# Two transformer blocks on one core: transfers of a recurrence queued by hand, weights asked for three blocks ahead, and a reworked quarter-product stage

## The chip, the cores and the metric

One of the eight cores of a Trainium2 chip runs the kernel. The metric is the device time of one execution in microseconds (us). TensorE is written PE (its weight loads PEld), VectorE DVE, ScalarE ACT, GpSimd POOL and SyncE SP. SP computes nothing: it issues transfers, in the order of its queue. ACT also issues transfers, between its computing instructions.

## The reference

Input x has 1024 tokens of 1024 features, all in float32. Two blocks follow each other.

```
h  = x + norm(mixer(norm(x)));  h = h + norm(w_down(gelu(conv(w_up.norm(h))_gate) * conv(..)_up))
mixer: p = xn @ w_in; a gated 3-tap convolution on 512 columns; on the rest a recurrence per head (8 heads of 64):
   S_t = S_(t-1) * w_t + (S_(t-1) . -kk_t) (kk_t a_t) + v_t k_t ;   y_t = S_t r_t
second block: sliding-window attention and forgetting attention, gates, w_mix_out,
   h = h + relu(u @ w_ff1)^2 @ w_ff2;  h = h + sigmoid(norm(h) @ w_ple_gate) * (p @ w_ple_proj);  norm(h)
```

## The kernel before, in words

**Dense products.** Activations are feature-major: a tile is 128 features by 512 tokens (one of two halves). Each float32 factor is split into a high and a low part (`split`: ACT writes the high part, DVE or POOL subtracts it), and a product is three matmuls: high by high, high by low, low by high. A weight block of 128 output columns (512 KB) is loaded by SP into one of two `wr` tiles (`raw_w`, L155), split into one of two `wh` and two `wl` tiles (`load_w`, L148) and used for 24 matmuls per half (`mm3`, L160). Each block asks for its weights when it starts.

**The first stage** is one TensorE order that `weave` writes by hand. Threads yield estimated TensorE time or a `gap` in us; the clock of `weave` runs the first thread in its list that is ready. The chain of the recurrence comes first, dense products fill in (`fill`, L1567 on). The other engines are ordered by the compiler's scheduler, from its own simulated times, with what was written first going first among what is ready. The recurrence has eight units (four pairs of heads by two halves). Unit i goes through

- `pre` (L552): five loads (sig, kt, aa, rt, vt) from DRAM, DVE and ACT work, two small sums on TensorE. `pre_thread` starts it when `solve` of unit i-1 is done;
- `solve` (L605): 32 products psA, masked by DVE into `am`; the small triangular blocks go to DRAM (d_l, L632) and come back copied to four groups of partitions (lt, L634); TensorE transposes (psB, psV) meanwhile; POOL inverts (`triangle`, L665, 62 multiplications and additions); the inverse goes to DRAM (d_m, four transfers, L656; d_n, L659) and back into `am` (L661). `solve` writes all these at once; it starts when the chain of unit i-2 is done;
- `chain` (L688): `weave` lets it start 35 us (`tri`) after `solve`; it loads `tr` from d_n (four transfers, L696), does 32 small products psR, then eight serial steps psX, psU, psH, psy, whose results go through DVE (xz, hb) and ACT (uv, hw);
- `post` (L769): a norm, then a gate `gg` loaded by SP.

**The quarter products.** In both feed-forward layers the last 17 (first) and 13 (second) pairs of weight blocks use seven products of half size in place of eight (`Quads`, L882). `operands` adds high and low parts of x back together on POOL (r, L904), forms four differences T1 to T4 on DVE (L907) and splits them. `weights` forms four sums and differences of a pair of weight blocks on POOL (s, L921) and splits five quarters. `pair` asks for its weights, then writes seven products of 12 matmuls into three banks of the tag `mm` (which has three), psX, psY and psZ, each taken out by ACT or added by DVE. The scheduler orders TensorE here.

Of the kernel before, what the change touches and what calls it, by code (L numbers as in the profile page):

```python
# [21 lines left out]
DC = math.exp(-0.5)  # L22
NEG = -1.0e30
ROW = 1 / 2210
GAP = dict(rsqrt=5.0, rstd=10.0, pre=16.0, pre2=10.0, tri=35.0, mix=3.5, hid=4.0, hop=1.2, x=1.4, u=0.9, h=1.2, sol=1.2, post=4.0, post2=4.0)
CH1 = (4, 4, 4, 2, 8)
# [51 lines left out]
class Kernel:  # L78
    def __init__(self, ctx, tc, vec):
        nc = self.nc = tc.nc  # L80
        self.in_block = False
# [66 lines left out]
    def load_w(self, wd, m, kb=8, cols=128, engine=None):  # L148

        raw = self.raw_w(wd, m, kb, cols)  # L150
# [19 lines left out]
    def dense(self, wd, m, x, then, kb=8, halves=(0, 1), cols=128, engine=None):  # L170
# [7 lines left out]
        self.in_block = False  # L178

    def dense32(self, wd, x, then, halves=(0, 1)):  # L180

        nc = self.nc
        yield until(lambda: not self.in_block)
        self.in_block = True
        raw = self.raw_w(wd, 0, NB, 32)
        w = self.wp.tile([128, NB, 64], F32R, tag="wh", name="wh")
        nc.scalar.copy(out=w[:, :, 0:32], in_=raw)
        nc.vector.tensor_tensor(out=w[:, :, 32:64], in0=raw, in1=w[:, :, 0:32], op=ALU.subtract)
        for hf in halves:
# [80 lines left out]

    def norm_to(self, src, gname, waits=(GAP["rstd"], GAP["rsqrt"]), pool=()):

# [3 lines left out]
        for j in range(NB):  # L276
# [81 lines left out]
def hs(hf):  # L358
    return slice(H * hf, H * hf + H)
# [14 lines left out]
class Mixer:  # L374
# [230 lines left out]
    def solve(self, st):  # L605
# [24 lines left out]
        d_l, d_m, d_n = self.d_l[ui], self.d_m[ui], self.d_n[ui]  # L630
        for b in range(2):
            nc.sync.dma_start(out=d_l[b].rearrange("u i t -> i u t"), in_=amu[32 * b:32 * b + 32, :, 32 * b:32 * b + 32])  # L632
        lt = k.q("lt", shape=(128, 32, 32))
        nc.sync.dma_start(  # L634
            out=lt.rearrange("p i t -> p (i t)"), in_=bass.AP(d_l.tensor, d_l.offset, [[0, 4], [1024, 32], [1, 1024]]))

# [14 lines left out]
        for p in range(2):  # L651
            nc.scalar.copy(out=uv[64:128, p:7 + p:2], in_=ps[64 * p:64 * p + 64])
        mt = self.triangle(lt)

        for r in range(4):
            nc.sync.dma_start(out=d_m[:, :, :, r].rearrange("b u s t -> (b u) s t"), in_=mt[32 * r:32 * r + 32])  # L656
        nm = k.a("mk", [128, 32, 8], name="nm")
        nc.gpsimd.tensor_copy(nm, mt.rearrange("p s t -> p t s"))
        nc.sync.dma_start(out=d_n.rearrange("r u t s -> (r u) t s"), in_=nm)  # L659
        for b in range(2):  # L660
            nc.sync.dma_start(  # L661
                out=amu[32 * b:32 * b + 32, :, 32 * b:32 * b + 32], in_=d_m[b].rearrange("u s r t -> (s r) u t"))
        return ar, am, bt, uv, wc, bv, d_n

# [23 lines left out]
    def chain(self, u, st):  # L688
        k = self.k
        nc = k.nc  # L690
        j, hf = u
        ar, am, bt, uv, wcs, bv, d_n = st
        amu = am.rearrange("p c h t -> p (c h) t")
        tr = k.a("tr", [64, 16, 4, 8])
        for r in range(4):
            nc.sync.dma_start(out=tr[0:32, :, r], in_=d_n[r, 0:16].rearrange("u t s -> t u s"))  # L696
        ps = k.ps("sc", (128, 16, 32), "psR")
# [184 lines left out]
class Quads:  # L882
# [6 lines left out]

    def operands(self, x):  # L890

# [74 lines left out]
class Ffn:  # L966
# [20 lines left out]
    def quads(self, js, q):  # L987
# [3 lines left out]
        pairs = self.up.pairs(js)  # L991
        for blocks, m0, m1 in pairs:
            cs = yield from q.pair(self.up.w, m0, m1)
            if blocks == pairs[-1][0]:
                self.hidden(0, (0, 1), "ws")
            self.up.pair(blocks, cs, keep)
# [474 lines left out]
def tile_blocks(ctx, tc, a, out):  # L1471
# [3 lines left out]
    ya_d, yb_d, h_d, h2_d, h3_d = d("ya_d", 4), d("yb_d", 4), d("h_d", 8), d("h2_d", 8), d("h3_d", 8)  # L1475
    sw_d, fx_d, gt_d, pj_d = d("sw_d", 4), d("fx_d", 4), d("gt_d", 16), d("pj_d", 8)
    xn = [{} for _ in range(NB)]

# [74 lines left out]
    def w_out_norm(src, hf):  # L1553
        yield from k.norm_add(src, "post_mix_g", a["x"], hf)
        k.spill(src, h_d, hf)
        yield gap(10.0)
        prs = yield from k.norm_to(src, "pre_ffn_g")
        for j, p in enumerate(prs):
# [3 lines left out]
    def krv(j, hf, names="krv"):  # L1562
        yield from mixer.krv(j, xn, (hf,), names)
        if "v" in names:
            done.add(("krv", (j, hf)))

    def fill():  # L1567
        kept = {}
        for token in ORDER:
# [38 lines left out]
    with tc.manual_schedule(engines={mybir.EngineType.PE}):  # L1608
        weave([*[chain_thread(i) for i in range(8)], post_thread(), pre_thread(), solve_thread(), norms(), norm0(), tail(),
               ple(), fill()])  # L1610
    k.a.close("mix")
    k.a.close("mixc")

    def ffn(ff, x, first, n):

        k.a.open("quad", QUAD, "right")
        q = Quads(k)
        q.operands(x)
# [7 lines left out]

    ffn(ff1, ff_in, 5, 22)

# [30 lines left out]
    for hf in range(2):  # L1659
        src = run(br.run(ys[hf], hf))  # L1660
        if hf == 0:
            ys.append(br.load(1))
        for j, p in enumerate(run(k.norm_to(src, "g_mlp_2"))):
            ff_in2[j][hf] = p
    run(ff2.ups(range(6), ff_in2, (0,)))
    k.a.close("q")
    k.a.close("att")
    ffn(ff2, ff_in2, 6, 32)
    pl_in = [{} for _ in range(NB)]
# [93 lines left out]
```

## Time and profile before

| | us |
|---|---|
| median of 3 runs (lowest, highest) | 3073.11 (3060.45, 3076.32) |
| the profiled execution's own time | 3067.94 |
| its span, first to last instruction | 3066.2 |
| TensorE busy in the span | 2883.5 (94%) |
| VectorE, ScalarE, GpSimd busy | 1822.0, 1260.5, 1003.5 |
| mean granted TensorE clock | 0.969 |

An instruction of an engine waits until what it needs is there, and everything behind it on that engine's queue waits too. `[idle before <-releaser]` in a timeline row is the time that the engine stood idle before the instruction, and who ended that wait. "Granted clock" is TensorE's clock as a share of 2.4 GHz; 0.5 is the lower level, 1.2 GHz.

### The profile page before, as it was taken

The numbers are of one execution on the slowest core, as the hardware profiler recorded it, in microseconds if no ns is written. First come the engines' busy times: TensorE is split into PE (matmuls) and PEld (weight loads), VectorE is DVE, ScalarE is ACT, GpSimd is POOL, SyncE is SP. The second block draws the span as 40 slices with busy tenths as digits, with TensorE's granted clock in tenths as the row PEclk, the third lists the DMA queues.
The fourth block names the chain that finished last, engine by engine and source line by source line (L and its number), as shares of the span: only waits on it lengthen the run. The fifth ranks groups of instructions, "written<-read, shape, count | busy, mean of one in ns | idle before, by whom it ended". The sixth has DMA issues, their size and how long they took to land.

```text
span 3066.2 us, 39452 instructions
## 1 busy us (share of the span) xinstructions
PE 2883.5 (94%) x14392; PEld 2316.4 (76%) x14392; DVE 1822.0 (59%) x3244; ACT 1260.5 (41%) x2187; POOL 1003.5 (33%) x1056
## 2 busy tenths in 40 slices
PE   7978889988998999999999999989998999999997
PEld 5756667766776777788778888877887787888886
DVE  6545555446886666445645776786667443544476
ACT  6433323234544444413335665564334443212342
POOL 2152433321345443003453446560026541000343
PEclk8988899999999999999999999999999999999998
DMA  6544332324422223423442322226543334433323
GB/s 209 173 116 121 106 99 75 90 66 158 162 87 83 82 76 100 147 66 96 152 163 64 91 73 73 73 66 223 165 134 114 117 110 145 172 98 102 97 89 131
DMA packets 188194, 349.72 MB, mean 114 GB/s; under 512 B 58712, under 2 KB 69464, under 8 KB 188000
## 3 DMA queue, kind: packets, MB, share of 16 engines
q1 hardware_dynamic: 146368, 268.51, 28.8%
q10 hardware_dynamic: 41632, 78.69, 7.0%
q8 instruction: 113, 1.85, 0.3%
q14 instruction: 81, 0.66, 0.1%
HBM read 265.05 MB, written 82.08 MB: 113 GB/s over the span
## 4 chain that ended last, share of the span: by engine, by line
PE 59%; DVE 6%; POOL 2%; issue 2%; DMA 2%; ACT 2%; ACTq 0%; SPq 0%; DVEq 0%; POOLq 0%
PE ps_mm L165 39%; PE psX L935 9%; PE psZ L935 5%; PE psY L935 2%; POOL s L921 1%; DVE sq L255 1%; PE pso L1326 1%; PE pst L1319 1%; DMA wr<-in_w_ff 1%; PE pso L1243 0%; PE pss L1280 0%; PE pss L1281 0%; DVE T L907 0%; DVE wl L146 0%; PE pst L1238 0%
## 5 line engine op out<-in xcount | busy, mean ns | idle before, releaser
L145 ACT CAST wh<-wr 128x1024 fp32r<-128x1024 f32 (+2 forms) x343 | 318.2, 928 | 647.2 <-PE ps_mm L165 534.2
L165 PE MATMUL ps_mm<-xh,wh 128*128 128x512 f32 x1344 | 547.2, 407 | 4.5 <-ACT xh L145 1.7
L165 PE MATMUL ps_mm<-xl,wh 128*128 128x512 f32 x1344 | 543.0, 404 | 1.8 <-DVE xl L146 1.8
L146 POOL TENSOR_TENSOR wl<-wr,wh 128x1024 fp32r<-128x1024 f32 (+1 forms) x109 | 255.2, 2342 | 853.6 <-ACT wh L145 671.2
L165 PE MATMUL ps_mm<-xh,wl 128*128 128x512 f32 x1344 | 370.5, 407 | 0.0
L165 PE MATMUL ps_mm<-hh,wh 128*128 128x512 f32 x864 | 343.2, 397 | 8.7 <-DVE acc L1029 3.8
L165 PE MATMUL ps_mm<-hl,wh 128*128 128x512 f32 x864 | 342.9, 397 | 0.0
L146 DVE TENSOR_TENSOR wl<-wr,wh 128x1024 fp32r<-128x1024 f32 (+2 forms) x234 | 250.5, 1071 | 107.2 <-PE ps_mm L165 45.8
L165 PEld LDWEIGHTS ps_mm<-xh,wh 128*128 128x128 f32 x1344 | 257.6, 192 | 62.4 <-issue 2.1
L165 PEld LDWEIGHTS ps_mm<-xl,wh 128*128 128x128 f32 x1344 | 257.5, 192 | 55.6 <-DVE xl L146 2.3
L165 PEld LDWEIGHTS ps_mm<-xh,wl 128*128 128x128 f32 x1344 | 251.1, 192 | 54.0
L1029 DVE TENSOR_TENSOR acc<-acc,ps_mm 128x512 f32<-128x512 f32 x176 | 120.6, 686 | 248.4 <-PE ps_mm L165 241.5
L165 PE MATMUL ps_mm<-hh,wl 128*128 128x512 f32 x864 | 233.8, 396 | 0.0
L677 POOL TENSOR_TENSOR pr<-mt,lt 128x60 f32<-128x60 f32 (+24 forms) x248 | 96.9, 391 | 328.7 <-DMA lt<-d_l 309.9
L165 PEld LDWEIGHTS ps_mm<-hh,wh 128*128 128x128 f32 x864 | 163.8, 190 | 48.5 <-DVE acc L1029 4.2
L165 PEld LDWEIGHTS ps_mm<-hl,wh 128*128 128x128 f32 x864 | 163.9, 190 | 38.2
L165 PEld LDWEIGHTS ps_mm<-hh,wl 128*128 128x128 f32 x864 | 163.4, 189 | 38.2
L921 POOL TENSOR_TENSOR s<-wr 128x512 f32<-128x512 f32 x60 | 90.2, 1503 | 272.0 <-DMA wr<-in_w_up 148.5
L255 DVE TENSOR_TENSOR sq<-sq 128x512 f32<-128x512 f32 x112 | 123.5, 1102 | 36.5 <-ACT sq L253 24.2
L904 POOL TENSOR_TENSOR r<-xh,xl 128x512 f32<-128x512 f32 x32 | 70.0, 2215 | 229.4 <-PE ps_mm L165 177.1
L1303 POOL TENSOR_SCALAR S<-S,sm 128x512 f32<-128x512 f32 (+3 forms) x96 | 119.2, 1253 | 73.8 <-DVE sm L1301 48.5
L805 DVE SCALAR_TENSOR_TENSOR ft<-c,vec,ft 128x1023 f32<-128x1023 f32 x68 | 92.1, 1355 | 40.6 <-ACT ft L803 40.4
(379 smaller groups left out, 5824.5 us busy)
## 6 DMA issues: line engine op xcount, KB each, us to landing
wr<-in_w_in SPq DMA_DIRECT2D x58, 512.0 KB, 4.0
wr<-in_w_up SPq DMA_DIRECT2D x54, 512.0 KB, 3.5
h<-hid SPq DMA_DIRECT2D x108, 256.0 KB, 4.2
wr<-in_w_ff SPq DMA_DIRECT2D x54, 512.0 KB, 3.5
wr<-in_w_in2g SPq DMA_DIRECT2D x32, 512.0 KB, 3.5
hid<-c ACTq DMA_DIRECT2D x26, 512.0 KB, 2.8
wr<-in_w_ff SPq DMA_DIRECT2D x48, 256.0 KB, 2.7
hid<-ft ACTq DMA_DIRECT2D x17, 512.0 KB, 2.6
```

Of the source, the lines that this page charges most:

```text
L145: self.nc.scalar.copy(out=pair[0], in_=src)
L146: (engine or self.nc.vector).tensor_tensor(out=pair[1], in0=src, in1=pair[0], op=ALU.subtract)
L165: self.nc.tensor.matmul(ps, lhsT=a[:, j, :cols], rhs=x[j][hf][part], start=i == 0, stop=i == 3 * kb - 1)
L255: self.nc.vector.tensor_tensor(out=sq, in0=acc, in1=sq, op=ALU.add)
L677: e.tensor_tensor(out=pr, in0=mt[:, :n, i:i + 1].to_broadcast([128, n, m]), in1=lt[:, i:i + 1, i + 1:].to_broadcast([128, n, m]), op=ALU.mult)
L805: nc.vector.scalar_tensor_tensor(out=t[:, i:], in0=src[:, :-i], scalar=c(2 - i), in1=t[:, i:], op0=ALU.mult, op1=ALU.add)
L904: nc.gpsimd.tensor_tensor(out=raw[n], in0=pr[0], in1=pr[1], op=ALU.add)
L921: nc.gpsimd.tensor_tensor(out=o, in0=x, in1=y, op=op)
L935: self.k.nc.tensor.matmul(ps, lhsT=a[:, j], rhs=x[j][part], start=start and i == 0, stop=i == 3 * half - 1, skip_group_check=True)
L1029: k.nc.vector.tensor_tensor(out=o, in0=o, in1=ps, op=ALU.add)
L1303: nc.gpsimd.tensor_scalar(out=s, in0=s, scalar1=sums[0], scalar2=None, op0=ALU.mult)
L1319: nc.tensor.transpose(pt[:, x], sc[i, e][kb // 4][:, c0:c0 + 128], k.ident)
```

## The change

It has three parts. **Weights:** `fill` writes a plan of its weight blocks; asking for one block also asks for the next ones, so that three stand ahead. **Recurrence:** the transfers are written at other places and tied on SP's queue behind the weight load written last (`queued`); the inverse's way back is a thread of its own; `pre` of unit i may start when `solve` of unit i-2 is done. **Quarters:** `norm_to` also stores x whole in DRAM, `operands` loads it instead of adding, two of four differences move to POOL, weights of the next pair are asked for before a pair's products, psY takes a bank of another tag, and TensorE follows the written order from the `ups` before them on.

```diff
-GAP = dict(... tri=35.0, ...)
+AHEAD = 3
+GAP = dict(... tri=3.0, ... dl=3.0, inv=28.0, back=4.0, ...)
...
     def load_w(self, wd, m, kb=8, cols=128, engine=None):
+        def get(wd, m):
+            if wd.shape[-1] == 32:
+                return self.fetch32(wd)
+            return self.fetch(wd, m, kb, cols, engine)
+        asked = [x for x in (self.ahead[:1] or self.plan[:1]) if x[0] is wd and x[1] == m]
+        if not asked:
+            return get(wd, m)
+        w = self.ahead.pop(0)[2] if self.ahead else get(*self.plan.pop(0))
+        while self.plan and len(self.ahead) < AHEAD:
+            nxt = self.plan.pop(0)
+            self.ahead.append((*nxt, get(*nxt)))
+        return w
...
-        self.nc.sync.dma_start(out=raw, in_=wd[m])
+        self.last_load = self.nc.sync.dma_start(out=raw, in_=wd[m])
+    def queued(self):
+        return self.tc.issue_after(getattr(self.last_load, "ins", self.last_load))
...
             self.split(x, pr, nc.gpsimd if j in pool else nc.vector)
+            if keep is not None:
+                nc.scalar.dma_start(out=keep[0][j][:, hs(keep[1])], in_=x)
...
-        for b in range(2):
-            nc.sync.dma_start(out=d_l[b]..., in_=amu[...])
-        lt = k.q("lt", shape=(128, 32, 32))
-        nc.sync.dma_start(out=lt..., in_=bass.AP(d_l.tensor, d_l.offset, [[0, 4], [1024, 32], [1, 1024]]))
+        with k.queued():
+            for b in range(2):
+                nc.sync.dma_start(out=d_l[b]..., in_=amu[...])
...
-        mt = self.triangle(lt)
-        for r in range(4):
-            nc.sync.dma_start(out=d_m[:, :, :, r]..., in_=mt[32 * r:32 * r + 32])
+        yield gap(GAP["dl"])
+        lt = k.q("lt", shape=(128, 32, 32))
+        with k.queued():
+            nc.sync.dma_start(out=lt..., in_=bass.AP(d_l.tensor, d_l.offset, [[0, 4], [1024, 32], [1, 1024]]))
+        return ar, am, bt, uv, wc, bv, self.triangle(lt), (d_m, d_n)
+    def back(self, st):
...
+        yield gap(GAP["inv"])
         nm = k.a("mk", [128, 32, 8], name="nm")
         nc.gpsimd.tensor_copy(nm, mt.rearrange("p s t -> p t s"))
-        nc.sync.dma_start(out=d_n..., in_=nm)
-        for b in range(2):
-            nc.sync.dma_start(out=amu[...], in_=d_m[b]...)
+        with k.queued():
+            for r in range(4):
+                nc.sync.dma_start(out=d_m[:, :, :, r]..., in_=mt[32 * r:32 * r + 32])
+            nc.sync.dma_start(out=d_n..., in_=nm)
+        yield gap(GAP["back"])
+        tr = k.a("tr", [64, 16, 4, 8])
+        with k.queued():
+            for b in range(2):
+                nc.sync.dma_start(out=amu[...], in_=d_m[b]...)
+            for r in range(4):
+                nc.sync.dma_start(out=tr[0:32, :, r], in_=d_n[r, 0:16]...)
+        return *st, tr
...
     def chain(self, u, st):
-        tr = k.a("tr", [64, 16, 4, 8])
-        for r in range(4):
-            nc.sync.dma_start(out=tr[0:32, :, r], in_=d_n[r, 0:16]...)
...
     def operands(self, x, x_d):
-            for n, pr in (("11", x[i][0]), ("12", x[i][1]), ("22", x[half + i][1]), ("21", x[half + i][0])):
-                raw[n] = k.t("r" + n, tag="ws")
-                nc.gpsimd.tensor_tensor(out=raw[n], in0=pr[0], in1=pr[1], op=ALU.add)
+            for n, j, hf in (("11", i, 0), ("12", i, 1), ("22", half + i, 1), ("21", half + i, 0)):
+                raw[n] = k.load(x_d[j], hf, "r" + n, "ws")
...
-                nc.vector.tensor_tensor(out=raw[n], in0=raw[a], in1=raw[b], op=ALU.subtract)
+                e = nc.gpsimd if n in ("T3", "T4") else nc.vector
+                e.tensor_tensor(out=raw[n], in0=raw[a], in1=raw[b], op=ALU.subtract)
...
-    def pair(self, wd, m0, m1):
-        w = self.weights(wd, m0, m1)
-        px, py, pz = [k.ps("mm", name=n) for n in ("psX", "psY", "psZ")]
+    def pair(self, w):
+        px, py, pz = [k.ps(tag, name=n) for tag, n in (("mm", "psX"), ("sc", "psY"), ("mm", "psZ"))]
...
     def quads(self, js, q):
-        for blocks, m0, m1 in pairs:
-            cs = yield from q.pair(self.up.w, m0, m1)
+        ws = [q.weights(self.up.w, *pairs[0][1:])]
+        for i, (blocks, _, _) in enumerate(pairs):
+            if i + 1 < len(pairs):
+                ws.append(q.weights(self.up.w, *pairs[i + 1][1:]))
+            cs = yield from q.pair(ws.pop(0))
...
     def pre_thread():
-            yield has(("krv", u), ("rate", u), *([("solve", i - 1)] if i > 1 else []))
+            yield has(("krv", u), ("rate", u), *([("solve", i - 2)] if i > 2 else []))
...
+    def back_thread():
+        for i in range(8):
+            yield has(("solve", i))
+            solved[i] = yield from mixer.back(solved[i])
+            done.add(("back", i))
     def chain_thread(i):
-        yield has(("solve", i))
+        yield has(("back", i))
...
     def ffn(ff, x, x_d, first, n):
-        run(ff.ups(range(first), x, (1,)))
-        run(ff.quads(range(first, n), q))
+        with tc.manual_schedule(engines={mybir.EngineType.PE}):
+            run(ff.ups(range(first), x, (1,)))
+            run(ff.quads(range(first, n), q))
```

## Rows read from the trace of the kernel before

**Rows 1.** Busy time by engine (share of the span, instructions), the page.

```profile
PE 2883.5 (94%) x14392; PEld 2316.4 (76%) x14392; DVE 1822.0 (59%) x3244; ACT 1260.5 (41%) x2187; POOL 1003.5 (33%) x1056
```

**Rows 2.** Busy time and granted clock in stretches, core 0 (x: instructions).

```profile
core 0: us, PE busy (x) PEld busy (x) DVE busy (x) ACT busy (x) POOL busy (x), PEclk, DMA share, GB/s
0.00:730.00 730.00, 621.62 (x4165) 481.81 (x4166) 381.75 (x817) 273.30 (x505) 222.33 (x583) 0.90 0.40 119
...
862.00:968.00 106.00, 95.24 (x393) 74.62 (x392) 81.30 (x101) 51.41 (x76) 47.16 (x30) 0.97 0.27 90
968.00:1248.00 280.00, 271.21 (x1162) 216.90 (x1161) 177.71 (x169) 130.20 (x178) 112.25 (x72) 1.00 0.25 81
...
2327.00:2415.00 88.00, 79.41 (x333) 63.00 (x333) 50.20 (x52) 38.96 (x62) 52.02 (x37) 0.98 0.31 104
2415.00:2600.00 185.00, 182.64 (x792) 148.21 (x790) 76.62 (x89) 76.38 (x111) 60.75 (x43) 1.00 0.34 117
```

**Rows 3.** TensorE's waits from 0 to 740 us: total, times, longest.

```profile
PE psH L745 <- ACT uv L742: 30.0, 6, 13.0
PE psB L643 <- DVE am L624: 16.1, 1, 16.1
PE psR L699 <- DMA tr<-d_n: 13.9, 3, 5.9
PE ps_mm L165 <- ACT wh L145: 12.1, 2, 8.1
PE psl L439 <- DVE wax L456: 8.1, 1, 8.1
```

**Rows 4.** Waits of SP's queue from 0 to 740 us.

```profile
SPq L656 <- POOL mt L680: 107.3, 7, 19.0
```

**Rows 5.** Timelines of SP (first two) and DVE about 180 us.

```profile
170.89 2.60 SPq L656 DMA_DIRECT2D d_m<-mt  x4
...
179.53 0.43 SPq L140 DMA_DIRECT2D sig<-d_sig  x1
...
183.00 0.43 DVE L564 TENSOR_SCALAR sig<-sig 128x512 f32<-128x512 f32 x1 [16.92 <-DMA sig<-d_sig]
```

**Rows 6.** Timeline of ACT and of its transfers about 231 us.

```profile
231.17 0.34 ACTq L443 DMA_DIRECT2D d_sig<-lo  x1
...
236.36 0.69 ACT L442 ACTIVATE lo<-psl,hw 128x512 f32<-128x512 f32 x1 [13.90 <-DMA am<-d_m]
```

**Rows 7.** One unit from lt to psR: timelines of SP, POOL and PE.

```profile
467.96 0.56 SPq L634 DMA_DIRECT2D lt<-d_l  x1
...
506.18 2.53 SPq L656 DMA_DIRECT2D d_m<-mt  x4
...
478.14 0.24 POOL L677 TENSOR_TENSOR pr<-mt,lt 128x31 f32<-128x31 f32 x1 [30.28 <-DMA lt<-d_l]
...
515.02 2.02 PE L699 MATMUL psR<-tr,am 32*32 32x32 f32 x32 [5.94 <-DMA tr<-d_n]
```

**Rows 8.** Busy time and granted clock just after that wait, columns of rows 2.

```profile
515.00:527.00 12.00, 11.92 (x98) 9.76 (x98) 4.12 (x6) 5.52 (x11) 0.00 (x0) 0.52 0.45 154
```

**Rows 9.** Transfers by issue: KB each, median us from issue to landing.

```profile
wr<-in_w_in SPq DMA_DIRECT2D x58, 512.0 KB, 4.0
```

**Rows 10.** Timeline of PE: one quarter product of two successive pairs.

```profile
1008.08 0.50 PE L935 MATMUL psZ<-T1h,S1h 128*128 128x512 f32 x1 [0.68 <-ACT c L962]
...
1028.40 0.50 PE L935 MATMUL psZ<-T1h,S1h 128*128 128x512 f32 x1 [0.68 <-ACT c L962]
```

**Rows 11.** POOL's sums of x (the page); from 968 to 1248 us: two DVE splits, POOL.

```profile
L904 POOL TENSOR_TENSOR r<-xh,xl 128x512 f32<-128x512 f32 x32 | 70.0, 2215 | 229.4 <-PE ps_mm L165 177.1
...
L146 DVE TENSOR_TENSOR S1l<-s,S1h 128x512 fp32r<-128x512 f32 x12 | 17.2, 1430 | 36.1 <-ACT S1h L145 36.1
...
L146 DVE TENSOR_TENSOR S4l<-s,S4h 128x512 fp32r<-128x512 f32 x12 | 8.1, 679 | 0.0
...
L921 POOL TENSOR_TENSOR s<-wr,s 128x512 f32<-128x512 f32 x12 | 15.6, 1300 | 0.9
```

More of the change, by code (lines that the diff above doesn't have):

```diff
@@ L23 @@
 NEG = -1.0e30
+AHEAD = 3
 ROW = 1 / 2210
-GAP = dict(rsqrt=5.0, rstd=10.0, pre=16.0, pre2=10.0, tri=35.0, mix=3.5, hid=4.0, hop=1.2, x=1.4, u=0.9, h=1.2, sol=1.2, post=4.0, post2=4.0)
+GAP = dict(rsqrt=5.0, rstd=10.0, pre=16.0, pre2=10.0, tri=3.0, mix=3.5, hid=4.0, hop=1.2, x=1.4, u=0.9, h=1.2, sol=1.2, dl=3.0, inv=28.0, back=4.0, post=4.0, post2=4.0)
 CH1 = (4, 4, 4, 2, 8)
@@ L80, in __init__ @@
         nc = self.nc = tc.nc
+        self.tc = tc
+        self.last_load = None
+        self.plan, self.ahead = [], []
         self.in_block = False
@@ L178, in dense, with fetch32 @@
         self.in_block = False
+    def fetch32(self, wd):
+        nc = self.nc
+        raw = self.raw_w(wd, 0, NB, 32)
+        w = self.wp.tile([128, NB, 64], F32R, tag="wh", name="wh")
+        nc.scalar.copy(out=w[:, :, 0:32], in_=raw)
+        nc.vector.tensor_tensor(out=w[:, :, 32:64], in0=raw, in1=w[:, :, 0:32], op=ALU.subtract)
+        return w
     def dense32(self, wd, x, then, halves=(0, 1)):
@@ L184, in dense32 @@
         self.in_block = True
[L185 to L188, printed above, removed]
+        w = self.load_w(wd, 0)
         for hf in halves:
@@ L269, in rstd_of, with norm_to @@
         return r
-    def norm_to(self, src, gname, waits=(GAP["rstd"], GAP["rsqrt"]), pool=()):
+    def norm_to(self, src, gname, waits=(GAP["rstd"], GAP["rsqrt"]), pool=(), keep=None):
         nc = self.nc
@@ L630, in solve @@
         d_l, d_m, d_n = self.d_l[ui], self.d_m[ui], self.d_n[ui]
[L631 to L635 removed]
+        with k.queued():
+            for b in range(2):
+                nc.sync.dma_start(
+                    out=d_l[b].rearrange("u i t -> i u t"), in_=amu[32 * b:32 * b + 32, :, 32 * b:32 * b + 32])
         bt = k.q("bt", shape=(128, 8, 128))
@@ L652, in solve @@
             nc.scalar.copy(out=uv[64:128, p:7 + p:2], in_=ps[64 * p:64 * p + 64])
[L653 to L656 removed]
+        yield gap(GAP["dl"])
+        lt = k.q("lt", shape=(128, 32, 32))
+        with k.queued():
+            nc.sync.dma_start(
+                out=lt.rearrange("p i t -> p (i t)"),
+                in_=bass.AP(d_l.tensor, d_l.offset, [[0, 4], [1024, 32], [1, 1024]]))
+        return ar, am, bt, uv, wc, bv, self.triangle(lt), (d_m, d_n)
+    def back(self, st):
+        k = self.k
+        nc = k.nc
+        *st, mt, (d_m, d_n) = st
+        amu = st[1].rearrange("p c h t -> p (c h) t")
+        yield gap(GAP["inv"])
         nm = k.a("mk", [128, 32, 8], name="nm")
         nc.gpsimd.tensor_copy(nm, mt.rearrange("p s t -> p t s"))
[L659 to L663 removed]
+        with k.queued():
+            for r in range(4):
+                nc.sync.dma_start(
+                    out=d_m[:, :, :, r].rearrange("b u s t -> (b u) s t"), in_=mt[32 * r:32 * r + 32])
+            nc.sync.dma_start(out=d_n.rearrange("r u t s -> (r u) t s"), in_=nm)
+        yield gap(GAP["back"])
+        tr = k.a("tr", [64, 16, 4, 8])
+        with k.queued():
+            for b in range(2):
+                nc.sync.dma_start(
+                    out=amu[32 * b:32 * b + 32, :, 32 * b:32 * b + 32], in_=d_m[b].rearrange("u s r t -> (s r) u t"))
+            for r in range(4):
+                nc.sync.dma_start(out=tr[0:32, :, r], in_=d_n[r, 0:16].rearrange("u t s -> t u s"))
+        return *st, tr
     def triangle(self, lt):
@@ L691, in chain @@
         j, hf = u
-        ar, am, bt, uv, wcs, bv, d_n = st
+        ar, am, bt, uv, wcs, bv, tr = st
         amu = am.rearrange("p c h t -> p (c h) t")
-        tr = k.a("tr", [64, 16, 4, 8])
-        for r in range(4):
-            nc.sync.dma_start(out=tr[0:32, :, r], in_=d_n[r, 0:16].rearrange("u t s -> t u s"))
         ps = k.ps("sc", (128, 16, 32), "psR")
@@ L888, in __init__, with operands @@
         self.x = {}
-    def operands(self, x):
+    def operands(self, x, x_d):
         k = self.k
@@ L991, in quads @@
         pairs = self.up.pairs(js)
-        for blocks, m0, m1 in pairs:
-            cs = yield from q.pair(self.up.w, m0, m1)
-            if blocks == pairs[-1][0]:
+        ws = [q.weights(self.up.w, *pairs[0][1:])]
[3 more added lines that the diff above has]
+            cs = yield from q.pair(ws.pop(0))
+            if i + 1 == len(pairs):
                 self.hidden(0, (0, 1), "ws")
@@ L1556, in w_out_norm @@
         yield gap(10.0)
-        prs = yield from k.norm_to(src, "pre_ffn_g")
+        prs = yield from k.norm_to(src, "pre_ffn_g", keep=(x1_d, hf))
         for j, p in enumerate(prs):
@@ L1565, in krv, with planned @@
             done.add(("krv", (j, hf)))
+    def planned():
+        w = a["w_in1"]
+        for token in ORDER:
+            what = token[0]
+            yield from {"R": [(w, 24)], "a": [(a["w2a2"], 0)], "G": [(a["w_in1t"], 0), (w, 25)], "g": [(a["g2"], 0)]}.get(
+                what) or [(w, 12 + 4 * "rkv".index(what) + int(token[2]))]
+        for j in range(4):
+            yield from [(w, j), (w, 8 + j), (w, 4 + j)]
+        yield from [(a["w_out"], m) for m in range(NB)]
     def fill():
+        k.plan = list(planned())
         kept = {}
@@ L1608, in tile_blocks @@
     with tc.manual_schedule(engines={mybir.EngineType.PE}):
-        weave([*[chain_thread(i) for i in range(8)], post_thread(), pre_thread(), solve_thread(), norms(), norm0(), tail(),
+        weave([*[chain_thread(i) for i in range(8)], post_thread(), back_thread(), pre_thread(), solve_thread(), norms(), norm0(), tail(),
                ple(), fill()])
@@ L1612, in tile_blocks, with ffn @@
     k.a.close("mixc")
-    def ffn(ff, x, first, n):
+    def ffn(ff, x, x_d, first, n):
         k.a.open("quad", QUAD, "right")
         q = Quads(k)
-        q.operands(x)
-        run(ff.ups(range(first), x, (1,)))
-        run(ff.quads(range(first, n), q))
+        q.operands(x, x_d)
+        with tc.manual_schedule(engines={mybir.EngineType.PE}):
+            run(ff.ups(range(first), x, (1,)))
+            run(ff.quads(range(first, n), q))
         k.a.close("quad")
@@ L1662, in tile_blocks @@
             ys.append(br.load(1))
-        for j, p in enumerate(run(k.norm_to(src, "g_mlp_2"))):
+        for j, p in enumerate(run(k.norm_to(src, "g_mlp_2", keep=(x2_d, hf)))):
             ff_in2[j][hf] = p
```

6 lines of the change are left out of this document (4 added, 2 removed).

## The prediction

> **What bounds the kernel now.** The busy times come first: TensorE is busy for 2883.5 of 3066.2 us [rows 1], 94%, so nothing but TensorE's idle time, its slow clock or its work can shorten the span. The change takes no matmul away. So the question is where TensorE stands still, and I read that by stage [rows 2]. The first 730 us, which hold the recurrence, have 621.62 us busy and a granted clock of 0.90: 108 us idle. The two stretches in which quarter products begin are the next: 106 us with 393 matmuls and 88 us with 333. The full rate is read from a steady pair: it lasts 20.32 us [rows 10], of which 0.68 us is idle, for 84 matmuls, so 19.64 / 84 = 0.234 us each. At that rate the two stretches would hold 453 and 376, so 60 and 43 are missing: 14 and 10 us. In steady state the first layer loses 0.68 us in each pair, about 14 times, 9.5 us; the second does 792 matmuls in 185 us, 0.234 us each, and loses nothing [rows 2].
>
> Whom TensorE waits for in the first stage is in its waits [rows 3]: 30.0 us for uv of ACT, 16.1 us in one wait for DVE's am, 13.9 us in three waits for tr. The 12.1 us at the start (first weights) and 8.1 us for wax are not touched. The three together, 60 us, have one origin, SP's queue. It stands 107.3 us at d_m, in seven of the eight units, because POOL has not finished the inverse [rows 4]. What is queued behind waits: sig of a later unit was issued at 179.53, right after the transfers that wait ended at 170.89 for; DVE stood 16.92 us for it at the head of its own queue [rows 5], and the masking of psA was behind. ACT is caught too: its transfer of a finished tile went out at 231.17 only, and ACT's next instruction had stood 13.90 us, ended by a transfer of the recurrence [rows 6]; uv was behind it. After a wait TensorE runs at its lower level for some time: after the 5.94 us at psR the granted clock was 0.52 over 12 us [rows 7, 8], which is up to 12 x 0.48 = 5.8 us of work lost.
>
> **Weights three ahead: 0 us by themselves.** There are still two `wr`, two `wh` and two `wl` tiles. A load three blocks ahead starts when the split of the block one ahead has freed its tile, which is when it starts now. What hides it: two loaded or split blocks, over 10 us of matmuls (24 x 0.234 = 5.6 us per block and half), against a landing of 4.0 us [rows 9]. If a split gets ahead of an eviction on ACT or DVE, one split's time is lost, and seldom; bounds 0 and +5 us.
>
> **Transfers behind the loads.** Each of the eight units issues 14 transfers on SP, as before (two d_l, lt, four d_m, d_n, two am, four tr). d_m is now written 28 us of `weave`'s clock after lt. TensorE's real time runs a little slower than that clock: in the unit of rows 7 it came to psR at 515.02 - 5.94 = 509.08, 41 us after lt's issue, where 38.7 are written (35 of tri and 3.7 of psB, psV and their gaps). So SP arrives at d_m some 30 us after lt was issued; the inverse ends 38 us after (467.96 to 506.18 [rows 7]). SP's wait becomes about 8 us in place of 107.3 / 7 = 15. Behind it stand weights that TensorE needs 10 us later. So:
> - am, 16.1 us: `pre` no longer waits for the `solve` just before it, so its five loads (0.43 us each on SP [rows 5]) are written before the d_m that held them. Gone: -16 us; bounds 0 and -16.
> - uv, 30.0 us: ACT is held half as long. I take -18; bounds 0 and -30.
> - tr, 13.9 us: here the change adds. From lt's issue to psR takes 515.02 - 467.96 = 47 us: 10.2 until POOL starts, 28.0 of inverse, 8.9 back through DRAM, none of it shortened. TensorE came there after 41; dl puts it 3 us of written time later, 44.5; a load three ahead may push lt back by some 3 us. So psR may wait 2.5 to 5.5 us in each of seven units, unless the chain before it ends later anyway, as it more often will, since `solve` no longer waits for `pre`. I take 2.5 x 7 = 17 against 13.9: +3; bounds -14 and +25.
> - the clock: fewer and shorter waits. These are ten waits [rows 3], each followed by up to 5.8 us of lost work, most by less since the shorter waits stop the clock less; I take 3 each, 30 in all, and a third less: -10; bounds 0 and -30.
>
> Sum for the recurrence: -16 - 18 + 3 - 10 = -41 us.
>
> Of that inverse path the lt transfer is the odd one: 512 KB in 10.2 us [rows 7], where a weight of the same size lands in 4.0 [rows 9]. The Trainium skill, page "DMA: Bandwidth & Descriptors", section "Rules for kernel authors", says that the slowest dimension of the access pattern sets how many DMA engines work, so that a leading broadcast of four copies keeps the transfer to four engines at most. lt's pattern begins with [0, 4] and is not changed, and the trace agrees with the rule: by it no place in the queue makes the 10.2 us shorter, and the sum above stays.
>
> **Quarters.** Taken out: 32 sums on POOL, 70.0 us [rows 11], 35 per layer. Added per layer: 16 stores on ACT's queue (0.34 us each as in rows 6, 5.4 us), 16 loads on SP (0.43 us, 6.9 us), 8.4 MB of traffic (in 106 us 79 GB/s over the 90 that flow there, with the DMA engines 27% busy [rows 2]), and eight differences on POOL, 1.3 us each like its sum of the same shape [rows 11], 10 us, for eight fewer on DVE. The sums stood in front of the first pairs' weights on POOL; with 25 us less of them the weights are ready while the `ups` before still run. Of the 14 + 10 us lost at the starts I take 15 back; bounds -24, and +10 if loads of x arrive late and TensorE, now in written order, cannot step around them.
>
> POOL's new work has a side to it. A DVE split takes 1.43 us where POOL's work runs beside it and 0.679 where it does not [rows 11]. The page "SBUF — State Buffer" of the Trainium skill, section "Who interferes with whom", has VectorE and GpSimd share a port pair under an exclusive lock. By it eight differences per layer would hold DVE for up to 10 us, but 35 us of sums held it before, so the sum would move the same way.
>
> In steady state psX no longer waits for a bank: five banks instead of three. 0.68 x 14 = 9.5 us; I take -8. The written order has its own price, which no row shows: psX is used four times in a pair, with one other product (12 x 0.234 = 2.8 us) between for its eviction. The bounds are 0 and one eviction's wait, 0.68 us, for each of 30 pairs, +20.
>
> **The sum** is made against the profiled execution's 3067.94 us (span 3066.2 and 1.7 around it), 0.2% under the median of 3073.11: -41 - 15 - 8 = -64, so 3004 us.
>
> **Rivals.**
> - *psR takes over the waits.* If lt goes out late in most units, psR waits 5.5 us in each, and clock is lost each time: 7 x (5.5 + 3) = 60 us, where am and uv gave back 34 and the old tr and its clock 20. The recurrence gains nothing, the quarters 23: 3045. For it: the 47 us, which nothing shortens. Against: `solve` starts earlier.
> - *All of it goes.* 60 us of waits, 20 of clock, 24 + 9.5 at the quarters, and little new: 3068 - 114 = 2954, or some 2945 if the last chain ends sooner. For it: one origin for all. Against: the inverse still needs 47 us.
> - *`pre` runs too far ahead (slower).* It allocates 14 tiles of a tag that has 14, and may now start while two more tiles of a unit not yet solved (vt, bv) are held. From the point where a load of `pre` waits on SP for a tile that only a later `post` frees, lt, d_m and tr stand behind it. One such wait costs what the sig wait cost, 16 us, and 3 of clock; in five or six units 100 us, against 64 gained: 3105. Against: four or five tiles are held when it starts, and its need at one time is nine or ten.
> - *Written order costs what it gives.* One eviction late in each pair, +20, late operands, +10, and the recurrence alone gains: 3068 - 41 + 30 = 3057, no change that can be told.
> - *The order on SP stays what it was*, because the transfers were already behind those loads. Then d_m still waits about 15 us, and only `pre` and the quarters gain: 3068 - 16 - 23 = 3029. It goes with the first rival.
>
> **Chances.** Forecast 0.47; psR, with the unchanged order, 0.22 (of it 0.20 faster by over 0.5%); all of it 0.13; written order 0.09; `pre` 0.09. A measurement of this kernel tells about 0.5%, 15 us, from no change. Faster: 0.47 + 0.20 + 0.13 = 0.80, less 0.02 for the forecast's own tail: 0.78. Same: 0.09 + 0.02 + 0.02 = 0.13. Slower: 0.09. The range leaves out `pre`, and the outer half of the case in which all goes: 2950 to 3060.
>
> **What the changed profile would show.** Right: SP's wait at d_m near 50 us in total instead of 107; no wait of DVE for sig; ACT's uv wait under 15 us; the first 730 us of work done by about 690; the POOL line of sums of x gone and loads of x in its place; pairs of the first layer near 19.7 us; over 440 matmuls in the first 106 us of quarters. Wrong: psR waiting in six or seven units, for tr; SP waiting for a tile of `pre` ahead of lt; TensorE waiting for c of ACT or DVE in every pair; a first stage as long as before with other names in its waits.

## The result and the profile after

The changed kernel takes 3031.17 us (median of 4, 3024.17 to 3035.48), the kernel before 3068.11 beside it: a ratio of 0.9877, 95% interval 0.984 to 0.9914. That is 37 us less, where 64 were forecast; the range of 2950 to 3060 held it. The profiled execution took 3035.48 us, with a span of 3033.7. As forecast, TensorE's work is the same and only its share of the span went up; this is the page's line of busy times for the changed kernel [rows 1]:

```profile
PE 2879.1 (95%) x14392; PEld 2314.8 (76%) x14392; DVE 1803.3 (59%) x3228; ACT 1262.4 (42%) x2187; POOL 972.8 (32%) x1040
```

The stretches of [rows 2], in the changed kernel:

```profile
0.00:730.00 730.00, 635.29 (x4229) 492.84 (x4230) 393.07 (x831) 282.45 (x518) 233.88 (x589) 0.91 0.42 124
862.00:968.00 106.00, 97.97 (x415) 77.01 (x415) 73.31 (x79) 50.42 (x75) 57.85 (x36) 1.00 0.26 87
968.00:1248.00 280.00, 275.37 (x1185) 222.90 (x1184) 176.50 (x173) 134.45 (x187) 107.98 (x66) 0.99 0.30 102
```

The first 730 us still hold 95 us of idle time. By landmarks: the last product of `w_out` ends at 755.6 us instead of 770.6, so the first stage gave 15 us. That is good to some 10 us only: in the two other profiles of the old first stage it ends at 774.4 and 781.7, in three others of the new one at 745.7 to 753.9. The first network's quarter products end at 1219.46 instead of 1251.24, 32 us earlier: 17 more. The second network's end at 2556.77 instead of 2592.03, so only 3.5 us more came after the first network; its steady pairs alternate between 22.11 and 16.64 us before, 19.38 on average, and take 19.37 after.

Whom TensorE waits for in the first stage, in the changed kernel [rows 3]:

```profile
PE psU L788 <- DVE xz L782: 15.4, 6, 8.9
PE psB L674 <- DVE am L656: 14.6, 1, 14.6
PE ps_mm L189 <- ACT wh L149: 11.6, 2, 9.0
PE ps_sp L276 <- DVE am L656: 8.7, 5, 5.9
PE psl L471 <- DVE wax L488: 8.1, 1, 8.1
PE psR L748 <- DMA tr<-d_n: 6.5, 2, 3.9
PE psH L794 <- ACT uv L791: 6.3, 5, 3.7
```

The wait for uv fell from 30.0 to 6.3 us and that for tr from 13.9 to 6.5. That for am stayed (14.6 against 16.1), and two others rose: psU from 6.1 to 15.4, ps_sp for am from 0.8 to 8.7.

SP's wait at d_m has a second row, which [rows 4] leave out. In the kernel before:

```profile
SPq L656 <- POOL nm L658: 20.1, 1, 20.1
```

So it stood 107.3 + 20.1 = 127 us there, in all eight units. As forecast, the wait fell by more than half, to 35.0 + 13.4 = 48 us:

```profile
SPq L704 <- POOL mt L732: 35.0, 5, 10.8
SPq L704 <- POOL nm L701: 13.4, 1, 13.4
```

But sig of the third unit is still behind the d_m that waits, and DVE still stands for it [rows 5]; in all, DVE's waits for sig rose from 22.9 us in three to 32.7 in five. Timelines of SP (first two) and DVE, changed kernel:

```profile
170.88 2.60 SPq L704 DMA_DIRECT2D d_m<-mt  x4
...
174.22 0.37 SPq L144 DMA_DIRECT2D sig<-d_sig  x1
...
177.62 0.43 DVE L596 TENSOR_SCALAR sig<-sig 128x512 f32<-128x512 f32 x1 [15.48 <-DMA sig<-d_sig]
```

And the earlier `pre` brought a wait of its own. Its tile ar takes a buffer that the running inverse still reads; DVE waits for POOL, xz is queued behind ar on DVE, and TensorE waits for xz. Timelines of DVE and PE, changed kernel:

```profile
313.62 0.69 DVE L618 TENSOR_TENSOR ar<-rt,W 128x512 f32<-128x512 f32 x1 [10.12 <-POOL pr L729]
...
315.56 0.71 PE L788 MATMUL psU<-xz,am 128*66 128x64 f32 x4 [8.94 <-DVE xz L782]
```

In steady state a pair of the first network takes 19.36 us (19.37 in most pairs) instead of 20.32, and the 0.68 us wait is gone [rows 10]. Timeline of PE, changed kernel:

```profile
1050.44 0.39 PE L984 MATMUL psZ<-T1h,S1h 128*128 128x512 f32 x1
...
1069.80 0.39 PE L984 MATMUL psZ<-T1h,S1h 128*128 128x512 f32 x1
```

The second to fifth pairs are slower than that, 20.83, 23.17, 22.32 and 24.66 us from one T4 product to the next; before, 26.27, 26.92 and then 20.32.

### The profile page after: what moved, and what is told of

Read it like the earlier page. It is cut to its first block, busy times and chain, and to the rows that moved or that the text cites. A ratio compares the mean times of both kernels' runs of the same rounds, so it can differ in the third digit from the quotient of the medians.

```text
span 3033.7 us, 39575 instructions
## 1 busy us (share of the span) xinstructions
PE 2879.1 (95%) x14392; PEld 2314.8 (76%) x14392; DVE 1803.3 (59%) x3228; ACT 1262.4 (42%) x2187; POOL 972.8 (32%) x1040
## 4 chain that ended last, share of the span: by engine, by line
PE 60%; DVE 5%; DMA 3%; POOL 2%; issue 2%; ACT 1%; SPq 0%; DVEq 0%; ACTq 0%; POOLq 0%
PE ps_mm L189 41%; PE psX L984 8%; PE psZ L984 4%; PE psY L984 2%; POOL s L970 2%; PE pso L1377 1%; PE pst L1370 1%; DVE sq L285 1%; DMA wr<-in_w_up 1%; DVE ft L854 0%; DMA wr<-in_w_ff 0%; PE pss L1331 0%; PE pso L1294 0%; PE pss L1332 0%; PE pst L1289 0%
## 5 line engine op out<-in xcount | busy, mean ns | idle before, releaser
L729 POOL TENSOR_TENSOR pr<-mt,lt 128x60 f32<-128x60 f32 (+24 forms) x248 | 90.3, 364 | 271.1 <-DMA lt<-d_l 252.2
L189 PE MATMUL ps_mm<-yh,wh 128*128 128x512 f32 x256 | 104.7, 411 | 5.1 <-ACT yh L149 4.8
```

The lines of the kernel that those rows point to most:

```text
L189: self.nc.tensor.matmul(ps, lhsT=a[:, j, :cols], rhs=x[j][hf][part], start=i == 0, stop=i == 3 * kb - 1)
L729: e.tensor_tensor(out=pr, in0=mt[:, :n, i:i + 1].to_broadcast([128, n, m]), in1=lt[:, i:i + 1, i + 1:].to_broadcast([128, n, m]), op=ALU.mult)
```

## The experiments

All ratios are to the kernel before, run beside them on the same chip. Not all the kernels ran on one chip, so they are set against each other by these ratios and by their profiles.

**The two halves alone.** First the kernel before with only the quarters' part (x whole in DRAM, weights a pair ahead, TensorE in written order, psY in another bank):

> The kernel before with the quarter-product part alone. Theory (two parts that add): the changed trace's quarter stages ended 17 us sooner relative to the stage before them (31.8 - 15 us in the first layer, 3.5 less 2.5 in the second), so the ratio is 0.994 (3068 to about 3050), the first stage (up to the last w_out product, 770.6 us before) unchanged within 3 us, steady pairs 19.37 us. Rival (the parts need each other: the quarters profit only because the first stage leaves its buffers sooner): less than 8 us, ratio 0.998.

Measured: 0.9954, interval 0.9939 to 0.9969. Then only the recurrence's part (plan, `queued`, `back`, the earlier `pre`, new gaps):

> The kernel before with the weights' plan and the recurrence's part alone. Theory (two parts that add): the first stage's last w_out product ends at about 756 us instead of 770.6, the rest as before: ratio 0.995 (about 3053). Rival (the parts need each other): nothing gained, 0.999 or more.

Measured: 0.9958, 0.9942 to 0.9975. Each half gives some 13 us of 3060, and the product, 0.9912, lies inside the changed kernel's interval, at its upper end: that they help or hinder each other can't be told.

**What in the quarters' part works.** First psY back in its old bank:

```diff
-        px, py, pz = [k.ps(tag, name=n) for tag, n in (("mm", "psX"), ("sc", "psY"), ("mm", "psZ"))]
+        px, py, pz = [k.ps(tag, name=n) for tag, n in (("mm", "psX"), ("mm", "psY"), ("mm", "psZ"))]
```

> The changed kernel with psY back in the tag of psX and psZ (three banks instead of five). Theory (the third bank of psX ended the 0.68 us wait of each pair): with TensorE in written order and three banks, psX of the next pair waits for the last eviction of the pair before; pairs of the first layer 20.1 us instead of 19.37, and of the second too, so 20 us slower than the changed kernel, ratio to before 0.994. Rival (the written order removed the wait, the banks do not matter): pairs stay at 19.4, ratio 0.988.

Measured: 0.9889, 0.9869 to 0.991, and steady pairs are still 19.37 us. The banks do nothing that can be told. Then each pair asks for its own weights, as before:

```diff
-        ws = [q.weights(self.up.w, *pairs[0][1:])]
-        for i, (blocks, _, _) in enumerate(pairs):
-            if i + 1 < len(pairs):
-                ws.append(q.weights(self.up.w, *pairs[i + 1][1:]))
-            cs = yield from q.pair(ws.pop(0))
+        for i, (blocks, m0, m1) in enumerate(pairs):
+            cs = yield from q.pair(q.weights(self.up.w, m0, m1))
```

> The changed kernel with each pair of quarters asking for its own weights when it starts, as before, all else kept. Theory (asked first, the next pair's splits stand on ACT in front of the evictions, and in the first pairs, where weights land late, the evictions wait with them): the first five pairs of the first layer lose 3 to 6 us together instead of 13, the second layer's 3 instead of 6, steady pairs stay at 19.4 us: ratio to before 0.985. Rival (the first pairs are late because the weights are, whoever asks; asked later it is worse): pairs 2 and 3 at 25 us and more as in the kernel before, ratio 0.990 or more.

Measured: 0.9898, 0.9876 to 0.992; the second to fifth pairs take 20.7, 23.23, 22.44 and 24.53 us as in the changed kernel. Asking a pair ahead does nothing that can be told. What is left was put alone into the kernel before:

```diff
-        run(ff.ups(range(first), x, (1,)))
-        run(ff.quads(range(first, n), q))
+        with tc.manual_schedule(engines={mybir.EngineType.PE}):
+            run(ff.ups(range(first), x, (1,)))
+            run(ff.quads(range(first, n), q))
```

> The kernel before, with one edit: TensorE in written order through the ups and quarter products of both networks; x is still summed on POOL and each pair still asks for its own weights. Theory: the written order alone carries the steady pair, 20.32 to 19.4 us in the first network, and with 14 such pairs, and the uneven pairs of the second network, nearly all that the quarters' part gave (ratio 0.9954): 0.995 to 0.997, with the first pairs starting no sooner. Rival: in written order TensorE must now stand for the sums of POOL that come late, which x whole in DRAM was there to prevent: the first pairs get longer by some 10 us in each network and the ratio is 0.999 to 1.003.

Measured: 0.9954, 0.9937 to 0.9972, the same as the whole quarters' part, with steady pairs of 19.37 us. So TensorE's written order is what gained there. The early pairs (21.44, 27.9, 20.6, 19.48) come to 89.4 us against 91.0 in the changed kernel: x whole in DRAM bought nothing that shows.

**What in the recurrence's part works.** The earlier `pre` undone:

```diff
-*([("solve", i - 2)] if i > 2 else [])
+*([("solve", i - 1)] if i > 1 else [])
```

> The changed kernel with pre of a unit again held until the solve just before it is done. Theory (the earlier pre lets solve start as soon as the chain two units before it ends, and that pays): from psR to psR of successive units it is 4 us longer in five units, DVE's wait for a tile that lt still holds (10.1 us) goes, and the first stage ends 5 to 12 us later: ratio to before 0.990 to 0.992. Rival (the earlier pre only takes tiles away from lt and the loads): the stage ends 5 us sooner, ratio 0.986.

Measured: 0.9983, 0.9969 to 0.9996, outside what was expected: nearly the whole gain of the change is lost without this line. The quarters' part, 0.9954 by itself, is still in this kernel, so what is left of the recurrence's part gives nothing without it, and rather costs some 9 us. The earlier `pre` by itself, in the kernel before, was not tried. The wait of ar is gone, and psR waits in seven units. TensorE's waits from 0 to 740 us, `pre` after the last solve:

```profile
PE psR L748 <- DMA tr<-d_n: 24.0, 7, 6.4
PE psB L674 <- DVE am L656: 15.5, 1, 15.5
```

Then the transfers no longer tied behind the loads (`queued` returns an empty context):

```diff
-        return self.tc.issue_after(getattr(self.last_load, "ins", self.last_load))
+        return ExitStack()
```

> The changed kernel without the ties on SP's queue; the written places, the gaps and the plan stay. Theory (the ties keep d_m behind the loads, since the scheduler's own times have the inverse done too early): SP's wait at d_m goes from 48 us back towards 107, TensorE's wait for uv back to 15 us or more, ratio 0.991 to 0.994. Rival (the written places and gaps do it): SP's wait within 15 us of 48, ratio 0.988.

Measured: 0.9924, 0.9904 to 0.9944; SP stands 96.9 + 15.7 us at d_m and psH waits 15.9 us. And no weights ahead (`k.plan = list(planned())` left out):

> The changed kernel with an empty plan: each block asks for its own weights, and the ties go to that block's own load. Theory (the plan by itself gives nothing, as the same two tiles are there; it only moves what the transfers are tied to, one block back in place of ahead): first stage within 6 us of the changed kernel, SP's wait at d_m longer by 10 to 30 us, ratio 0.987 to 0.991. Rival (asking three ahead brings weights earlier): TensorE's waits for split weights grow by over 15 us, ratio 0.994 or more.

Measured: 0.9919, 0.9898 to 0.994; SP 118.7 + 14.5 us at d_m, psH 28.3 us. Without the one or the other SP stands at d_m about as long as in the kernel before (113 and 133 us against 127), so both are needed for that. What they are worth in time is not clear: some 13 us come back, but the intervals overlap with the changed kernel's. The seven steps from unit to unit (told of below) take 452.8 and 449.0 us, against 435 to 445 in the four profiles that have the whole recurrence's part and 459.3 in the kernel before. With SP's wait as long as ever, most of the chain's gain may thus stay.

**Does SP's wait set the time?** The way back is written 36 instead of 28 us after lt:

```diff
-GAP = dict(..., dl=3.0, inv=28.0, back=4.0, ...)
+GAP = dict(..., dl=3.0, inv=36.0, back=4.0, ...)
```

> The changed kernel with d_m and d_n written 36 us after lt in place of 28. Theory: SP's wait at d_m falls from 48 us to under 10, but what is left of it costs little, since the weights behind it are asked for early, and the eight us come back at psR, where tr is now later: psR waits in most units, 20 to 30 us in all, the ratio to the kernel before is 0.988 to 0.994 (the changed kernel: 0.9877). Rival: SP's wait still sets the time, and the ratio goes to 0.982 to 0.985.

Measured: 0.9993, 0.9979 to 1.0008. SP's wait at d_m went down to 18.1 us, sig of the third unit went out at 156.13, ahead of d_m, and the wait of psB for am is gone. The forecast's chain of causes was cured, and the kernel is as slow as before the change. Theory and rival both missed it: the loss is far more than psR's 12.5 us of waiting. What rose is the time between units. The unit's psR matmuls, listed by the query on that tile (first and last start), in the kernel before, the changed kernel and this one, a fence for each:

```profile
L699 PE MATMUL psR<-tr,am x256: 218/231/258, 189.5 to 648.8; 32*32 32x32 f32 x128
```

```profile
L748 PE MATMUL psR<-tr,am x256: 210/231/258, 191.3 to 636.4; 32*32 32x32 f32 x128
```

```profile
L748 PE MATMUL psR<-tr,am x256: 212/230/236, 190.7 to 653.9; 32*32 32x32 f32 x128
```

Seven steps from unit to unit take 459.3, 445.1 and 463.2 us (the last start is that of the last unit's last psR, so each figure holds 1.8 us too much). The last product of `w_out` ends 121.8, 119.2 and 129.6 us after the last psR. In the other eleven profiles that distance is 118 to 126 us, while the seven steps take 404 to 465: the second half of `w_out` starts when `post` of all eight units is done. The first stage ends a nearly fixed time after the recurrence, and the recurrence is a chain: its steps, not the sum of TensorE's waits, are what a change must shorten. Eight us more of written distance in each unit made the chain 18 us longer.

The steps are not alike. Those of the kernel before take 70.4, 64.9, 66.4, 62.3, 61.5, 63.7 and 68.3 us, those of the changed kernel 61.3, 80.1, 60.3, 63.3, 54.4, 63.4 and 60.6. The second, to the third unit, got 15 us longer, and it takes 74 to 90 us in every kernel with the earlier `pre`, against 57 to 71 in the others. What holds it is open; those 15 us are as much as the first stage gained.

**The transfer of lt.** It is the longest step of that chain that does no arithmetic. In place of one transfer whose pattern begins with a broadcast of four, four transfers of 32 partitions each, first in the changed kernel:

```diff
-            nc.sync.dma_start(
-                out=lt.rearrange("p i t -> p (i t)"),
-                in_=bass.AP(d_l.tensor, d_l.offset, [[0, 4], [1024, 32], [1, 1024]]))
+            for r in range(4):
+                nc.sync.dma_start(
+                    out=lt[32 * r:32 * r + 32].rearrange("p i t -> p (i t)"),
+                    in_=d_l.rearrange("b u i t -> (b u) (i t)"))
```

> The changed kernel with lt loaded by four transfers of 32 partitions each instead of one whose pattern begins with a broadcast of four. Theory (the broadcast keeps the transfer to few DMA engines): POOL's triangle starts 4 to 6 us after lt's first issue instead of 9 to 15, SP's wait at d_m falls from 48 us to under 15, DVE's wait for sig of unit 2 from 15.5 to about 10 us, and the first stage ends 10 us sooner: ratio to before 0.984. Rival (all four copies read the same rows of DRAM, and that is what is slow): landing as now, ratio 0.988.

Measured: 2992.18 us, 0.9785, 0.9761 to 0.981: faster than both kernels, by more than was expected. From the first issue to the inverse's start it takes 5.8 us on average instead of 11.1, and the chain 404.3 us instead of 445.1; psR with four transfers:

```profile
L749 PE MATMUL psR<-tr,am x256: 212/230/257, 187.1 to 591.4; 32*32 32x32 f32 x128
```

Then the same edit, with nothing of the change, in the kernel before:

> The kernel before, with nothing of the change, and lt loaded by four transfers of 32 partitions each. Theory: lt's own time is what holds the recurrence, whatever the queue's order, since SP stands at d_m from the end of lt's issue to the end of the inverse: each of seven units loses some 5 us of its 15 there, SP's wait at d_m falls from 107 to about 70 us, and the gain is most of what the same edit gave the changed kernel (some 25 us): ratio 0.990 to 0.994. Rival: only the new order of the queue lets a shorter lt through (in the kernel before, pre waits for the solve just before it, and the wait only moves to am and uv): SP's wait falls, but the ratio is 0.997 to 1.000. A third outcome, a ratio near 0.985, would say that the old single transfer slowed others too, by the engines that it held.

Measured: 3018.27 us, 0.9853, 0.9827 to 0.9879: this edit alone gives about what the whole change gave, and the change is worth some 20 us more beside it (0.9785 against 0.9853). Two rows of one of its units, timelines of SP and POOL, to set beside [rows 7]:

```profile
440.84 1.71 SPq L635 DMA_DIRECT2D lt<-d_l  x4
...
446.07 0.24 POOL L679 TENSOR_TENSOR pr<-mt,lt 128x31 f32<-128x31 f32 x1 [29.50 <-DMA lt<-d_l]
```

And its psR:

```profile
L701 PE MATMUL psR<-tr,am x256: 210/230/236, 186.3 to 610.2; 32*32 32x32 f32 x128
```

From lt to the inverse 5.2 us instead of 10.2 (means of eight units: 4.9 and 10.8), so 5.9 x 7 = 41 us less in seven steps; the chain is 459.3 - 423.9 = 35 us shorter, and the time 45. The chain's gain is accounted for by lt itself, and the end of the first stage moves with it, from 770.6 to 734.5 us. The other 9 us I can't place: in these two profiles they lie between the quarter products of the two networks (1087.2 and 1076.8 us), a stretch that the edit doesn't touch and that takes 1076 to 1082 us in all the others.

While hardly anything but lt moves, the 16 DMA engines are busy for a share of 0.25, four engines' worth, at 76 GB/s in the kernel before, and for 0.94 at 252 GB/s with four transfers. Columns of [rows 2], the kernel before and this one:

```profile
410.00:414.00 4.00, 3.38 (x21) 2.50 (x19) 1.29 (x4) 1.57 (x3) 0.00 (x0) 1.00 0.25 76
```

```profile
381.00:383.00 2.00, 2.00 (x17) 1.73 (x15) 0.93 (x3) 0.73 (x2) 0.00 (x0) 1.00 0.94 252
```

I had named a ratio near 0.985 as a sign that the single transfer slows others too. It does: in three units SP issues gg, 256 KB, right behind lt, and it lands after 10.8 us in the kernel before and 4.1 in this one; DVE's wait for it falls from 12.1 to 1.9 us. What that is worth in the whole was not measured by itself. Transfers by issue from 250 to 420 us, the same two kernels:

```profile
gg<-d_g SPq DMA_DIRECT2D x3, 256.0 KB, 10.8
```

```profile
gg<-d_g SPq DMA_DIRECT2D x3, 256.0 KB, 4.1
```

**Both together with a later way back**, four transfers and `inv=32.0`:

> The changed kernel with lt in four transfers, and d_m and d_n written 32 us after lt in place of 28. SP's wait at d_m was 28 us in all with four transfers and 28 us; four us more in each of eight units should leave some 5. Theory: that wait is already harmless, and the time stays within 0.3% of the four transfers alone (ratio 0.976 to 0.982). Rival: it still holds sig (12.2 us) and am (11.4 us) back, and the ratio goes to 0.972 to 0.975.

Measured: 0.9834, 0.981 to 0.9857: slower than four transfers with 28, against theory and rival. SP's wait at d_m is down to 0.4 us, and the chain is longer by 26 us, near the 4 x 7 = 28 us more of written distance. But it isn't 4 us in each step: 13 of the 26 us lie in the one from the fourth to the fifth unit (58.4 and 71.5 us) and 6 in the one from the sixth to the seventh. What holds those steps was not found. Here too sig of the third unit went out ahead of d_m (156.88 and 169.01), and the wait of psB for am is gone. psR in this kernel:

```profile
L749 PE MATMUL psR<-tr,am x256: 210/230/236, 179.2 to 609.6; 32*32 32x32 f32 x128
```

Whether a way back written sooner than 28 us after lt beats 2992 us was not tried.

## Why the prediction was right in direction and short in size

**SP's wait at d_m: right**, 48 us against "near 50", though with the row that was left out it came from 127 and not from 107. The plan and the ties are what did it (113 us without the ties, 133 without the plan). But the price put on it was wrong. "The three together, 60 us, have one origin, SP's queue" is the sentence that fell: with four transfers of lt in the kernel before, SP stands 70.4 + 16.8 us at d_m and the first stage is 36 us shorter; with a way back at 36 us it stands 18.1 and the first stage is 13 us longer than before; without the plan it stands as long as before and the chain is still 10 us shorter. That the time fell in the forecast's direction and into its range is thus in part luck: what shortened the recurrence was in the change, but not for the reason given.

**am, -16: failed.** 14.6 of 16.1 us are still there. The step held that the five loads of `pre` would be written before the d_m that held them; in the third unit they still came after the d_m at 170.88, and went ahead of it only in the two kernels whose way back was written later, and both are slower than the same kernel with 28 us.

**uv, -18: undersized.** 30.0 fell to 6.3, within the bound of -30. **tr, +3: wrong sign**, 13.9 fell to 6.5; psR did not take over the waits. That rival describes instead the kernel with `pre` after the solve (24.0 us in seven waits). What the forecast lacked is the 17 us that rose at psU and at ps_sp. One of them, 8.9 us at psU, is the rival "`pre` runs too far ahead" in small, with another tile than I named: not one of the 14 of that tag, but ar, in a buffer still held by the inverse.

**The clock, -10:** TensorE's idle time in the first 730 us fell from 108.4 to 94.7 us, 13.7 of the 15 us of the first stage. So the clock gave 1 or 2 us as far as this shows (0.91 against 0.90). Together the recurrence's part was to give 41 us and gave 13 to 15.

**The step that failed** is thus the choice of view. I added up waits of TensorE by name, and called the earlier `pre` a matter of am alone. The chain from psR to psR, 457.5 us in seven steps without the 1.8 us too much, was in the same trace: 65.4 us a step, of which I had 47 from lt to psR written down with the words "none of it shortened", and used it only to price psR's waits. In the changed kernel a step is 63.3 us, and 66.2 with `pre` after the solve. The earlier `pre` shortens the chain by letting the next unit's psA and am be made before psR of the unit at hand: in the changed kernel psA of the fourth, sixth and eighth unit starts 8 to 13 us before that psR, where from the third unit on it starts 2 to 7 us after it in the kernel before and with `pre` after the solve. Timelines of PE, psR of the fifth and psA of the sixth unit, first in the kernel before, then in the changed kernel:

```profile
453.52 2.03 PE L699 MATMUL psR<-tr,am 32*32 32x32 f32 x32
...
456.89 1.28 PE L619 MATMUL psA<-ar,bk 64*128 64x128 f32 x10 [0.22 <-ACT yc L777]
```

```profile
444.57 1.16 PE L651 MATMUL psA<-ar,bk 64*128 64x128 f32 x16
...
456.20 1.00 PE L748 MATMUL psR<-tr,am 32*32 32x32 f32 x14
```

Without that line nearly all the gain is gone; that it is enough by itself is not shown.

**The page's rule on lt held.** No place in the queue made the transfer shorter: 11.1 us on average in the changed kernel, 10.8 before. With a pattern of 32 partitions outermost in place of the broadcast it takes about half, and the share of busy DMA engines is 0.94 in place of 0.25. The Trainium skill's page "DMA: Bandwidth & Descriptors", section "Rules for kernel authors", asks for an outermost dimension that is a multiple of 16 and gives at most four engines for a leading broadcast of four; both agree with these rows. The prediction cited it and left it at "the sum above stays", where it pointed at the best edit.

**The quarters: -23 forecast, -14 measured.** The steady pair gained 0.96 us where 0.68 was forecast, for another reason than the one given: five banks were credited, and with the old bank the gain stays; the written order alone does it. That order's own price, feared as a rival at 20 us, did not come: no wait of TensorE is listed from 1020 to 1200 us of the changed kernel. The starts, -15, are where the rest is missing: 415 matmuls stand in the first 106 us of quarters, where over 440 were forecast, and 393 before. The written order gives what is to be had, and neither x in DRAM nor the earlier weights add to it. Of the 8.0 us of idle time that are left there, 6.2 are waits for evictions on ACT. TensorE's waits from 862 to 968 us, changed kernel:

```profile
PE psX L984 <- ACT c L998: 4.5, 4, 1.7
PE psX L984 <- ACT c L1002: 1.7, 2, 1.1
```

POOL's eight differences per network against sums taken off it made no difference that can be told either: with the sums still there (written order alone) the ratio is the same 0.9954.

## What to carry to other kernels

Where a recurrence runs beside filler work, measure its step from unit to unit first: if the stage ends a fixed time after the last unit, only what shortens the step counts, and a stalled queue or a waiting engine counts only as far as it lengthens that step. A distance in time written into a hand-made order is paid in that chain, though not in proportion: here four us more per unit cost 26 in one kernel, and eight cost 18 in another. And a transfer that takes twice as long as another of its size deserves an edit before the queue around it does.

## What the runs showed of the hardware

One 512 KB transfer whose pattern starts with a broadcast of four took 9 to 15 us from issue to the first use in the changed kernel; the same bytes in four transfers of 128 KB, issued one behind the other in about 1.7 us, took 4 to 8 in all. The one transfer kept a share of 0.25 of the 16 DMA engines busy, the four 0.94, and a load issued right behind landed after 10.8 us and 4.1. In the kernel before this edit alone took off 1.5% of the time (0.9853).
